# A matrix product by nested seven-product schemes: one more product in quarters, and two measures of b22 moved

## The chip, the cores and the metric

One core of a Trainium2 chip runs the whole kernel. The metric is the device time of that core in microseconds (us); lower is better. Times below are for one execution unless they are called a median.

## The reference

```
a, b: float32, 4096 x 4096;  alpha: 0.01
x = a @ b
out = where(x > 0, x, alpha * x)
```

## The kernel before

**Seven products instead of eight.** Both matrices are cut into regions of the output of 1024 x 1024. A region is named (g, j): g counts 1024 rows of A (0 to 3), j counts 1024 columns of B (0 to 3). Region (0,0) is computed plainly at the start. Each of the 15 others is computed by Winograd's form of Strassen's scheme: the rows are split into two halves h of 512, the columns into two halves nt of 512, and the inner dimension of 4096 into two halves of 2048, each of which is held as two tiles k. From these come seven products of a 512 x 2048 block with a 2048 x 512 block, in this order (`PRODUCTS`): a11, a12, s2, s3, s1, a22, s4 on the side of A, where s1 to s4 are sums of blocks of A made by VectorE once per g (`sum_a`; s3 is made in the place of the block a21). On the side of B the sums are made in every region by `b_sum` (line 575), in place. A product is `product(n, banks, first)`, line 789: 64 matmuls of 128x128 by 128x512, two tiles k, eight chunks c, four row tiles mt, into four PSUM banks. Banks y take products one, three, five and seven, banks z products two, four and six; between them the accumulated values are copied by ScalarE (`keep`, line 802) or added by VectorE (line 946) to tiles c in SBUF, passed through the leaky step (line 310) and stored by `leave`.

**Quarters.** In the regions with g > 0 that bring in no A (`in_quarters`), the sixth and seventh products are split once more by the same scheme, into seven quarter products of 16 matmuls of 128x128 by 128x256 (`quarter_product`, line 739), and in all of these but the first of a group (`in_fourth`) the fourth is too (`fourth_in_quarters`). A quarter product needs further sums. On the side of B they are made by VectorE in each region: `t3_of_b` (line 668, in place) and `sums_of_b` (lines 674, 676, 678: tq 2, 4 and 1). On the side of A they are made once per group: those of s4 and a22 in the group's first region (`sums_of_a`, line 688) and stored to DRAM (`kept_q`); those of s3 by `sums_of_s3` (line 722), three of which stay in the rooms of the quarters x21 of a22, s4 and s3 (`s3_rooms`), while the fourth, sx4, goes to DRAM (`kept_s3`). The quarters x21 that are overwritten in this way are stored first (`keep_x21`, line 704) and loaded back (`load_x21`, line 710) for the regions that use the whole blocks again.

**The order of regions.** Group 0: (0,1), (0,2), (0,3). Group 1: (1,2), (1,0), (1,3), (1,1). Group 2: (2,2), (2,0), (2,3), (2,1). Group 3: (3,2), (3,0), (3,1), (3,3). The last region of groups 0 to 2 also brings in A for the next group (`turning`). For each quadrant (h, half) of the next A, four pieces n are fetched by POOL's DMA queue (`fetch_a`, line 132, four DMAs of 128 KB for a piece, float32 rounded to float16 on the way), turned by VectorE (line 141), and squared by ScalarE for a measure of their range (`square_a`, line 594). The pieces pass through the pool a16, which has three buffers. A quadrant can be turned only when the block that it replaces has had its last product: (0,0) during product two, (0,1) during products three and four, (1,0) from product five on, (1,1) in product seven. Then VectorE makes the next s1 and s2 (line 545).

**Order and waits.** The order of instructions on each engine is the order of the program text (a manual schedule); each engine and each DMA queue runs its own list in order, and waits on semaphores. Tiles of a pool are reused in the order in which they come free. The pool x holds three large tiles, in turn s1, s2 and s4 of a group; in the regions in quarters the tile `q` takes the place of s2 after the third product, and s2 is loaded again from DRAM (`load_s2`).

**Measures.** The kernel checks the ranges of its inputs. For each block of B and A a `Measure` squares it on ScalarE in four parts (line 230) and sums and folds the squares on VectorE (lines 239 to 263). Where a measure stands is given by tables: `EARLY`, `MEASURED` (the entries: one in the middle of the first two products; a list of late ones after the third product; a fifth and a sixth for after those products) and `IN_ROOM`, for those that use the place of the next s2 instead of buffers of a16. The last region judges the statistics (`judge`); a result out of range would send the kernel into a plain loop at its end, which these inputs do not use.

Of the kernel before, what the change touches and what calls it, by code (L numbers as in the profile page):

```python
# [8 lines left out]
P = 128  # L9
DT = mybir.dt.float16  # L10
# [37 lines left out]
def kernel(  # L48
# [524 lines left out]
    def b_sum(to, x0, x1, op):  # L573
        f = lambda t: t.rearrange("p c n -> p (c n)")
        nc.vector.tensor_tensor(f(to), f(x0), f(x1), op)  # L575

    def measure(i, which, x, y, room=None):

        if which:
            tiles = [have_b[i, 2 * x + k, y] for k in ((1, 0) if regions[i][0] else (0, 1))]  # L580
        else:
            tiles = [at[regions[i][0], x, 2 * y + k] for k in range(2)]
        parts = halves(tiles[0]) + halves(tiles[1])
        if tiles[0] is first_a:
            return MeasureFirst(which, parts, None)
        return Measure(which, parts, not which, room)

    junk = small_pool.tile([P, NT], BF16, name="junk")
    rows_made = []
# [12 lines left out]
    def judge(line):  # L602
# [29 lines left out]
        (1, 0): [B11], (1, 3): [B11], (2, 0): [B12, B21], (2, 3): [B21], (2, 1): [B12], (3, 1): [B11, B21],  # L632
    }
    MEASURED = {
        (0, 1): (None, [A11], B12, B11), (0, 2): (B21, [B22, A22], B12, A12),
        (3, 0): (B22, [], None, None),
    }
    IN_ROOM = {(0, 3): B22, (1, 1): B22}

    PRODUCTS = [("a11", 0, 0), ("a12", 1, 0), ("s2", 0, 0), ("s3", 0, 1), ("s1", 0, 0), ("a22", 1, 0), ("s4", 1, 1)]  # L640

# [5 lines left out]
    kept_s2 = dram_pool.tile([2, P, KC * RM], DT, name="kept_s2")  # L647
    kept_q = {name: dram_pool.tile([4, P, QUARTER], DT, name=f"kept_q{name}") for name in ("a22", "s4")}
    kept_s3 = dram_pool.tile([P, QUARTER], DT, name="kept_s3")
    kept_x21 = {name: dram_pool.tile([P, QUARTER], DT, name=f"kept_x{name}") for name in ("a22", "s4", "s3")}  # L650
    side = 0

    def a_quarter(t):
# [72 lines left out]
    def s3_rooms(g):  # L726
        return {1: x21(g, "a22"), 2: x21(g, "s4"), 3: x21(g, "s3")}
# [5 lines left out]
    def quarter_product(xq, yq, to, first=False, by_row=False, banks=1):  # L733
        order = [(c, m) for c in range(KC) for m in range(2)]
        if by_row:
            order = [(c, m) for m in range(2) for c in range(KC)]
        for c, m in order:
            rows = slice(m * P, (m + 1) * P)
            nc.tensor.matmul(  # L739
                to[m], xq[:, c // 2, rows, c % 2], yq[:, c, :],  # L740
                start=first and c == 0 and m < banks, stop=c == KC - 1, skip_group_check=True,
            )
# [27 lines left out]
    for i, (g, j) in enumerate(regions):  # L770
# [33 lines left out]

        def fourth_in_quarters(banks, tq, sx):

            pairs, kept = new_c(side)
            b = quarters_of_b(i, 0, 1)
            x = quarters_of_a(g, "s3")
            one, other, third, fourth = banks  # L810
            t = lambda n: b_quarter(tq[n])
            block = lambda r, n: pairs[r][:, :, n * HALF:(n + 1) * HALF]
            quarter_product(x[0, 1], b[1, 0], into(fourth), True)
            quarter_product(x[0, 0], b[0, 0], into(one), True)
            nc.scalar.copy(block(0, 0), pair(one))
            quarter_product(sx[4], b[1, 1], into(other), True)
            quarter_product(x[1, 1], t(4), into(third), True)
            nc.scalar.copy(block(1, 0), pair(third))
            quarter_product(sx[2], t(2), into(one))
            nc.scalar.copy(block(0, 1), pair(one))  # L820
            quarter_product(sx[1], t(1), into(third), True)
            nc.scalar.copy(block(1, 1), pair(third))
            quarter_product(sx[3], b[0, 1], into(one))
            return pairs, kept, [(block(r, n), pair(bank)) for r, n, bank in (
                (0, 0, fourth), (0, 1, other), (0, 1, third), (1, 0, one), (1, 1, one))]

# [117 lines left out]
        def add(acc, banks):  # L944
            for to, bank in zip(acc, banks):
                nc.vector.tensor_add(to, bank, to)  # L946

        def leave(pairs, h, nt):
            for r, t in enumerate(pairs):
                leaky(t.rearrange("p m n -> p (m n)"))  # L950
                for m in range(2):
                    nc.sync.dma_start(place(g, h, 2 * r + m, j, nt), t[:, m, :])
# [19 lines left out]
        def square_a(h, half, n):  # L972
            square_rows(coming[h, half][n][1].held[0], n, coming["rows", h, half])
            if n == MT - 1:
                rows_made.append(coming["rows", h, half])

        def bring_a(h, half, some=range(MT)):
            if turning:
                for n in some:
                    fetch_a(h, half, n)  # L980
                    coming[h, half][n][1]()
                    square_a(h, half, n)

        y = [new_bank(ybank + mt) for mt in range(MT)]
        z = [new_bank(zbank + mt) for mt in range(MT)]
# [41 lines left out]
        if first_of_group:  # L1027
            sum_a(g, "s3")
            if g:
                sum_a(g, "s4")  # L1030
        if turning and g:
            load_x21(g, "s3")
        bring_a(0, 0, range(3 if g else 4))

        product(1, z, True)
# [19 lines left out]
            sum_a(g, "s4")  # L1055
        for k in ks:
            b_sum(B(1, 0, k), B(1, 0, k), B(0, 0, k), SUB)
        if first_of_group and g:
            keep_x21(g, "s3")
            keep_x21(g, "s4")  # L1060
            sums_of_a(g, "s4", new_a16)
        if not g:
# [3 lines left out]
        if late_ones:  # L1066
            late_ones[0].begin()
        u2_pairs, u2 = keep(y, 1 - side)
        if in_quarters:
            t = x_pool.tile([P, 4, QUARTER], DT, name="q", tag="x")  # L1070
        if in_fourth:
            tq[1] = t[:, 3]
            sums_of_b(quarters_of_b(i, 0, 1), tq, (1,))
        for k in ks:
            b_sum(B(0, 0, k), B(1, 1, k), B(0, 0, k), SUB)
        if g:
            bring_a(0, 1, range(3))
        if late_ones:
            late_ones[0].end()
        if in_quarters and first_of_group:  # L1080
# [2 lines left out]
            keep_x21(g, "a22")  # L1083

        z = [new_bank(zbank + mt) for mt in range(MT)]
        if in_fourth:
            v_pairs, v, parts = fourth_in_quarters(z, tq, {**s3_rooms(g), 4: a_quarter(sx4)})
            for to, bank in parts:
                nc.vector.tensor_add(to, bank, to)
            sq = {n: t[:, 3] if n == 4 else new_a16() for n in (1, 2, 3, 4)}  # L1090
            load_sums("a22", sq, (1, 2, 3, 4))
        else:
            product(3, z, True)
            v_pairs, v = keep(z, side)
        if in_quarters:
            tq = {2: t[:, 0], 1: t[:, 1], 4: t[:, 2]}
        fetch_b(i + 1, [(0, 1)], (1, 0) if in_fourth else ks)
        in_room = None
        if turning:
            room = new_s(g + 1, "s2").rearrange("p k c m e -> p (k c m e)").bitcast(BF16)  # L1100
            if (g, j) in IN_ROOM:
                in_room = measure(i, *IN_ROOM[g, j], room.rearrange("p (n w) -> p n w", n=4))
                in_room.begin()
                in_room.end()
            if g:
                bring_a(0, 1, [3])
            note_rows(1)
            for n in range(3):
                fetch_a(1, 0, n)
            coming[1, 0][0][1]()  # L1110
            square_a(1, 0, 0)
            fetch_a(1, 0, 3)
            load_x21(g, "a22")
            load_x21(g, "s4")
# [6 lines left out]
        if in_quarters:  # L1121
            t3_of_b(quarters_of_b(i, 1, 0))
            sums_of_b(quarters_of_b(i, 1, 0), tq)
            t3_of_b(quarters_of_b(i, 1, 1))
            for to, more in zip(u2_pairs, v_pairs):
                f = lambda t: t.rearrange("p m n -> p (m n)")
                nc.vector.tensor_add(f(to), f(to), f(more))
            if final:
                good = next(judged)

# [7 lines left out]
            leave(v_pairs, 1, 1)  # L1138
        if turning:
            for n in range(1, MT):  # L1140
                coming[1, 0][n][1]()
                square_a(1, 0, n)
            note_rows(1)
        if fifth:
            fifth = measure(i + 1, *fifth)
# [2 lines left out]
        fetch_b(i + 1, [(0, 0)], ks)  # L1148

        if not in_quarters:  # L1150
            product(5, z, False)
            add(u2[::-1], z[::-1])
        fetch_b(i + 1, [(1, 0)], (1, 0) if in_quarters else ks)
        bring_a(1, 1, range(3))
# [101 lines left out]
```

## Time and profile before

| what | before |
|---|---|
| median of 3 runs | 1549.6 us (1549.58 to 1549.91) |
| the profiled execution | 1550.65 us |
| its span, first to last instruction | 1548.9 us |
| PE (TensorE matmul) busy | 1530.1 us, 99% |
| DVE (VectorE) busy | 1138.8 us, 74% |
| ACT (ScalarE) busy | 425.1 us, 27% |
| mean granted TensorE clock | 0.997 |
| DMA, mean over the span | 222 GB/s |

A line of a timeline has start, duration, engine, line of the kernel, operation, output and input, shapes and count, and in brackets the idle time before it and what ended it. A line of waits has the waiting engine and line, whom it waited for, the total in us, how often and the longest. In the chain of waits each line has the start, the duration and the work that held the end at that time; "issue" is time for which the profile shows no wait. The start of a region can be read from the timeline of PE: (1,2) begins at 412.87, (1,1) at 699.70, (2,2) at 796.39, (2,1) at 1073.89, (3,2) at 1170.59 and (3,3) near 1448.14.

### The profile page before, as it was taken

The page shows a single profiled execution, that of the slowest core. Times are in us where ns is not written, and L with a number is a line of the kernel's source. Part 1 is how long each engine was busy: PE and PEld are TensorE (multiplying, and loading weights), DVE is VectorE, ACT ScalarE, POOL GpSimd, SP SyncE. Part 2 cuts the span into 40 slices and gives each one's busy share as a digit, 9 for nine tenths or more (in the row PEclk, how much of TensorE's full clock was granted, in tenths as well). Part 3 has the DMA queues.
Part 4 walks back from the last instruction along what each step waited for, and adds up shares of the span by engine and source line. Part 5 has one row for each costly group of instructions (what it writes and reads, how often), then busy time and mean ns, then how long its engine had stood idle before and what let it go on. Part 6 is the DMA issues. An engine that isn't in the chain of part 4 may idle for free.

```text
span 1548.9 us, 21600 instructions
## 1 busy us (share of the span) xinstructions
PE 1530.1 (99%) x8571; PEld 838.1 (54%) x8571; DVE 1138.8 (74%) x1179; ACT 425.1 (27%) x730; POOL 282.5 (18%) x458
## 2 busy tenths in 40 slices
PE   9999999999998999999999999999999999999997
PEld 4444444444445557574444747657444475746656
DVE  4368757767697786767669798686958768787486
ACT  2201224646510312103650041312543103041110
POOL 5641110142201011013220201110430110101100
PEclk9999999999999999999999999999999999999999
DMA  9999995997979969599798989959899895949934
GB/s 247 186 214 196 237 285 160 181 191 156 244 287 267 262 150 269 144 284 282 148 265 289 284 197 195 281 147 325 168 277 280 210 268 136 288 169 187 272 116 139
DMA packets 207361, 343.90 MB, mean 222 GB/s; under 512 B 18961, under 2 KB 150289, under 8 KB 197266
## 3 DMA queue, kind: packets, MB, share of 16 engines
q0 software_dynamic: 136704, 129.00, 52.4%
q1 hardware_dynamic: 63922, 187.86, 33.0%
q10 hardware_dynamic: 6624, 25.56, 4.5%
q8 instruction: 69, 1.13, 0.3%
q14 instruction: 42, 0.34, 0.1%
HBM read 361.76 MB, written 107.48 MB: 303 GB/s over the span
## 4 chain that ended last, share of the span: by engine, by line
PE 69%; DVE 3%; DMA 2%; ACT 1%; issue 1%; POOL 0%; DVEq 0%; ACTq 0%
PE ps L789 47%; PE ps L739 21%; DMA a<-in_a_dram 1%; DVE b L575 1%; DVE s L545 1%; DMA kept_qs<-q 0%; ACT junk L594 0%; ACT s L230 0%; DVE c L310 0%; DVE a L545 0%; DVE a L141 0%; DVE c L946 0%; DVE q L688 0%; POOL a L132 0%; DVE c L937 0%
## 5 line engine op out<-in xcount | busy, mean ns | idle before, releaser
L789 PE MATMUL ps<-b,a 128*128 128x512 f16 x2752 | 598.9, 379 | 0.4 <-DVE c L946 0.4
L789 PE MATMUL ps<-b,s 128*128 128x512 f16 x2240 | 491.8, 380 | 5.8 <-DVE b L575 5.8
L789 PEld LDWEIGHTS <-a 128*128 128x128 f16 x2752 | 269.2, 98 | 323.7 <-issue 1.2
L789 PEld LDWEIGHTS <-s 128*128 128x128 f16 x2240 | 219.7, 98 | 271.0 <-DVE b L575 6.3
L575 DVE TENSOR_TENSOR b<-b 128x4096 f16<-128x4096 f16 x104 | 234.9, 2287 | 64.1 <-DMA b<-in_b_dram 58.9
L519 POOL DMA_DIRECT2D b<-in_b_dram x160 | 118.8, 747 | 876.9 <-PE ps L739 316.8
L802 ACT COPY c<-ps 128x512 f32<-128x512 f32 x172 | 88.8, 595 | 477.0 <-PE ps L789 407.0
L141 DVE STREAM_TRANSPOSE a<-a 128x512 uint32<-128x512 uint32 (+2 forms) x120 | 126.8, 1104 | 90.5 <-DMA a<-in_a_dram 90.3
L132 POOL DMA_DIRECT2D a<-in_a_dram x252 | 137.7, 552 | 263.3 <-ACT junk L594 99.9
L594 ACT ACTIVATE junk<-a 128x512 bf16<-128x512 f16 x192 | 121.2, 631 | 89.7 <-DMA a<-in_a_dram 76.6
L739 PEld LDWEIGHTS <-q 128*128 128x128 f16 x1392 | 136.2, 98 | 15.8
L310 DVE SCALAR_TENSOR_TENSOR c<-c 128x1024 f32<-128x1024 f32 (+1 forms) x121 | 141.4, 1209 | 4.4 <-ACT c L802 4.2
L946 DVE TENSOR_TENSOR c<-ps,c 128x512 f32<-128x512 f32 x142 | 88.8, 682 | 59.7 <-PE ps L789 46.3
L230 ACT ACTIVATE sq<-b 128x2048 bf16<-128x2048 f16 x56 | 104.3, 1910 | 55.2 <-DVE sq L239 40.7
L282 PE MATMUL ps<-b,a 128*128 128x512 f16 x512 | 112.8, 379 | 1.9 <-DVE part L321 0.8
L739 PEld LDWEIGHTS <-a 128*128 128x128 f16 x1040 | 101.8, 98 | 15.4
L739 PE MATMUL ps<-b,q 128*128 128x256 f16 x752 | 88.1, 273 | 0.0
L282 PEld LDWEIGHTS <-a 128*128 128x128 f16 x512 | 49.7, 98 | 62.9 <-issue 3.0
L887 ACT COPY c<-ps 128x512 f32<-128x512 f32 x9 | 5.3, 587 | 277.1 <-PE ps L739 156.9
L739 PE MATMUL ps<-b,a 128*128 128x256 f16 x656 | 77.2, 273 | 0.0
L840 DVE TENSOR_TENSOR c<-ps,c 128x512 f32<-128x512 f32 x80 | 52.3, 684 | 15.9 <-PE ps L739 15.9
L739 PEld LDWEIGHTS <-s 128*128 128x128 f16 x592 | 57.9, 98 | 6.7
(112 smaller groups left out, 880.8 us busy)
## 6 DMA issues: line engine op xcount, KB each, us to landing
b<-in_b_dram POOLq DMA_DIRECT2D x168, 512.0 KB, 12.1
out_dram<-c SPq DMA_DIRECT2D x240, 256.0 KB, 5.8
a<-in_a_dram POOLq DMA_DIRECT2D x244, 128.0 KB, 5.7
b<-kept SPq DMA_DIRECT2D x20, 1024.0 KB, 8.9
q<-kept_qs ACTq DMA_DIRECT2D x40, 512.0 KB, 7.7
s<-kept_s SPq DMA_DIRECT2D x18, 1024.0 KB, 7.3
q<-kept_qa SPq DMA_DIRECT2D x28, 512.0 KB, 7.1
b<-kept_last SPq DMA_DIRECT2D x12, 1024.0 KB, 11.3
```

Source lines behind the costliest of these rows:

```text
L132: nc.gpsimd.dma_start(a16[32 * q:32 * q + 32], src.rearrange("(g i) w -> i g w", i=32))
L141: nc.vector.transpose(part.rearrange("p c m e -> p c (m e)").bitcast(U32) .rearrange("p c (g i) -> p g c i", i=32), src[:, :, i * n:(i + 1 ...
L230: nc.scalar.activation(to, self.parts[n], SQUARE)
L282: nc.tensor.matmul(ps, a_cols(at[0, h, u], c, mt, (h, u) == (0, 0)), bt[0, u, nt][:, c, :], start=first, stop=last,)
L310: nc.vector.scalar_tensor_tensor(t, t, alpha, t, op0=MULT, op1=MAX if alpha <= 1 else MIN)
L519: nc.gpsimd.dma_start(t[:, c:c + 4, :], b_rows(j, u, c, 4, nt, g > 0))
L575: nc.vector.tensor_tensor(f(to), f(x0), f(x1), op)
L594: nc.scalar.activation(junk, piece[:, q, :], SQUARE, accum_out=to[:, 4 * n + q:4 * n + q + 1])
L739: nc.tensor.matmul(to[m], xq[:, c // 2, rows, c % 2], yq[:, c, :], start=first and c == 0 and m < banks, stop=c == KC - 1, skip_group_chec ...
L789: nc.tensor.matmul(banks[mt], a_cols(t, c, mt, t is first_a), B(half, nt, k)[:, c, :], start=first and (k, c) == todo[0], stop=(k, c) == t ...
L802: nc.scalar.copy(kept[mt], banks[mt])
L946: nc.vector.tensor_add(to, bank, to)
```

## The change

- In the two later turning regions, (1,1) and (2,1), the fourth product is made of quarters too. The tile `q` is now taken in every region with g > 0; in these two it holds tq 2, 4, 1 and sx4, and is given back before the next group's s2 takes that room. sx4 is loaded from `kept_s3`; its quarter product is the last of the seven there. VectorE makes t3 and the three sums of B around the end of the third product, adds five blocks from PSUM to the tiles v afterwards, and adds v to u2 (`add_v`); the sixth product then starts afresh in its banks.
- The fetches of the pieces (0,1) 0 to 2 of the next A are issued before the third product, and are turned and squared after the fourth has been issued.
- x21 of s3 is no longer stored in the groups' first regions, nor loaded in (1,1) and (2,1).
- The two measures in the room of s2 (B22 in (0,3) and in (1,1)) are gone with `IN_ROOM`; B22 is measured as a second late one in (0,1), and in the middle of (3,3).

```diff
     MEASURED = {
-        (0, 1): (None, [A11], B12, B11), (0, 2): (B21, [B22, A22], B12, A12),
-        (3, 0): (B22, [], None, None),
+        (0, 1): (None, [A11, B22], B12, B11), (0, 2): (B21, [B22, A22], B12, A12),
+        (3, 0): (B22, [], None, None), (3, 3): (B22, [], None, None),
     }
-    IN_ROOM = {(0, 3): B22, (1, 1): B22}
...
@@ fourth_in_quarters
             nc.scalar.copy(block(0, 0), pair(one))
-            quarter_product(sx[4], b[1, 1], into(other), True)
+            if not turning:
+                quarter_product(sx[4], b[1, 1], into(other), True)
             quarter_product(x[1, 1], t(4), into(third), True)
...
             quarter_product(sx[3], b[0, 1], into(one))
+            if turning:
+                quarter_product(sx[4], b[1, 1], into(other), True)
...
+        def add_v():
+            for to, more in zip(u2_pairs, v_pairs):
+                f = lambda t: t.rearrange("p m n -> p (m n)")
+                nc.vector.tensor_add(f(to), f(to), f(more))
...
+        def turn_a_in(h, half, n):
+            coming[h, half][n][1]()
+            square_a(h, half, n)
...
-        if turning and g:
-            load_x21(g, "s3")
         bring_a(0, 0, range(3 if g else 4))
...
         for k in ks:
             b_sum(B(1, 0, k), B(1, 0, k), B(0, 0, k), SUB)
+        if turning and g:
+            t3_of_b(quarters_of_b(i, 0, 1))
+            for n in range(3):
+                fetch_a(0, 1, n)
         if first_of_group and g:
-            keep_x21(g, "s3")
             keep_x21(g, "s4")
...
         u2_pairs, u2 = keep(y, 1 - side)
-        if in_quarters:
+        if g:
             t = x_pool.tile([P, 4, QUARTER], DT, name="q", tag="x")
         if in_fourth:
             tq[1] = t[:, 3]
             sums_of_b(quarters_of_b(i, 0, 1), tq, (1,))
+        elif turning and g:
+            tq, sx4 = {2: t[:, 0], 4: t[:, 1], 1: t[:, 2]}, t[:, 3]
+            sums_of_b(quarters_of_b(i, 0, 1), tq, (2, 4, 1))
+            nc.sync.dma_start(sx4, kept_s3)
         for k in ks:
             b_sum(B(0, 0, k), B(1, 1, k), B(0, 0, k), SUB)
-        if g:
-            bring_a(0, 1, range(3))
...
-        if in_fourth:
+        if in_fourth or turning and g:
             v_pairs, v, parts = fourth_in_quarters(z, tq, {**s3_rooms(g), 4: a_quarter(sx4)})
+            if turning:
+                for n in range(3):
+                    turn_a_in(0, 1, n)
             for to, bank in parts:
                 nc.vector.tensor_add(to, bank, to)
+            if turning:
+                add_v()
...
         if turning:
-            room = new_s(g + 1, "s2").rearrange("p k c m e -> p (k c m e)").bitcast(BF16)
-            if (g, j) in IN_ROOM:
-                in_room = measure(i, *IN_ROOM[g, j], room.rearrange("p (n w) -> p n w", n=4))
-                in_room.begin()
-                in_room.end()
+            new_s(g + 1, "s2")
...
         if not in_quarters:
-            product(5, z, False)
+            product(5, z, g > 0)
             add(u2[::-1], z[::-1])
```

More of the change, by code (lines that the diff above doesn't have):

```diff
@@ L575, in b_sum, with measure @@
         nc.vector.tensor_tensor(f(to), f(x0), f(x1), op)
-    def measure(i, which, x, y, room=None):
+    def measure(i, which, x, y):
         if which:
@@ L585, in measure @@
             return MeasureFirst(which, parts, None)
-        return Measure(which, parts, not which, room)
+        return Measure(which, parts, not which)
     junk = small_pool.tile([P, NT], BF16, name="junk")
@@ L649 @@
     kept_s3 = dram_pool.tile([P, QUARTER], DT, name="kept_s3")
-    kept_x21 = {name: dram_pool.tile([P, QUARTER], DT, name=f"kept_x{name}") for name in ("a22", "s4", "s3")}
+    kept_x21 = {name: dram_pool.tile([P, QUARTER], DT, name=f"kept_x{name}") for name in ("a22", "s4")}
     side = 0
@@ L980, in bring_a @@
                     fetch_a(h, half, n)
-                    coming[h, half][n][1]()
-                    square_a(h, half, n)
+                    turn_a_in(h, half, n)
         y = [new_bank(ybank + mt) for mt in range(MT)]
@@ L1085 @@
         z = [new_bank(zbank + mt) for mt in range(MT)]
-        if in_fourth:
+        if in_fourth or turning and g:
             v_pairs, v, parts = fourth_in_quarters(z, tq, {**s3_rooms(g), 4: a_quarter(sx4)})
+            if turning:
+                for n in range(3):
+                    turn_a_in(0, 1, n)
             for to, bank in parts:
                 nc.vector.tensor_add(to, bank, to)
-            sq = {n: t[:, 3] if n == 4 else new_a16() for n in (1, 2, 3, 4)}
-            load_sums("a22", sq, (1, 2, 3, 4))
+            if turning:
+                add_v()
         else:
@@ L1094 @@
             v_pairs, v = keep(z, side)
+        if in_fourth:
+            sq = {n: t[:, 3] if n == 4 else new_a16() for n in (1, 2, 3, 4)}
+            load_sums("a22", sq, (1, 2, 3, 4))
         if in_quarters:
             tq = {2: t[:, 0], 1: t[:, 1], 4: t[:, 2]}
-        fetch_b(i + 1, [(0, 1)], (1, 0) if in_fourth else ks)
-        in_room = None
+        fetch_b(i + 1, [(0, 1)], (1, 0) if in_fourth else (0, 1) if turning and g else ks)
         if turning:
-            room = new_s(g + 1, "s2").rearrange("p k c m e -> p (k c m e)").bitcast(BF16)
-            if (g, j) in IN_ROOM:
-                in_room = measure(i, *IN_ROOM[g, j], room.rearrange("p (n w) -> p n w", n=4))
-                in_room.begin()
-                in_room.end()
+            new_s(g + 1, "s2")
             if g:
@@ L1109 @@
                 fetch_a(1, 0, n)
-            coming[1, 0][0][1]()
-            square_a(1, 0, 0)
+            turn_a_in(1, 0, 0)
             fetch_a(1, 0, 3)
@@ L1124 @@
             t3_of_b(quarters_of_b(i, 1, 1))
-            for to, more in zip(u2_pairs, v_pairs):
-                f = lambda t: t.rearrange("p m n -> p (m n)")
-                nc.vector.tensor_add(f(to), f(to), f(more))
+            add_v()
             if final:
@@ L1140 @@
             for n in range(1, MT):
-                coming[1, 0][n][1]()
-                square_a(1, 0, n)
+                turn_a_in(1, 0, n)
             note_rows(1)
```

## The prediction

> **What bounds the kernel now.** I read the page first, then who waits for whom on PE, then the PE timeline around the one long wait, then the chain of waits backwards from it.
>
> ```profile
> PE 1530.1 (99%) x8571; PEld 838.1 (54%) x8571; DVE 1138.8 (74%) x1179; ACT 425.1 (27%) x730; POOL 282.5 (18%) x458
> ```
>
> That is the page's busy time by engine; next, PE's longest wait (total, times, longest), and PE's timeline around it:
>
> ```profile
> PE ps L789 <- DVE b L575: 5.8, 1, 5.8
> ```
>
> ```profile
> 454.31 0.67 PE L789 MATMUL ps<-b,a 128*128 128x512 f16 x2
> ...
> 474.91 16.63 PE L789 MATMUL ps<-b,s 128*128 128x512 f16 x64 [5.78 <-DVE b L575]
> 491.38 1.91 PE L739 MATMUL ps<-b,a 128*128 128x256 f16 x16
> ```
>
> PE is the bound and waits long only once: 5.78 us before the fifth product of region (1,2). The clock was halved after it. In the table by windows (length, busy time of PE, PEld, DVE, ACT and POOL, then clock, DMA share, GB/s):
>
> ```profile
> 472.00:474.00 2.00, 0.00 (x0) 0.00 (x0) 2.00 (x2) 0.00 (x0) 0.34 (x1) 0.87 1.11 330
> 474.00:476.00 2.00, 1.09 (x3) 0.43 (x4) 2.00 (x2) 0.00 (x0) 0.00 (x0) 0.50 1.22 220
> ```
>
> The chain of waits says what made the wait, and gives the price of both kinds of product:
>
> ```profile
> 373.04 7.21 ACT s L230 x4
> 380.24 4.36 issue
> ...
> 395.35 17.07 DMA a<-in_a_dram
> ...
> 464.84 7.71 DMA kept_qs<-q
> 472.55 0.02 issue
> 472.57 2.30 DVE b L575
> 474.87 0.05 issue
> 474.91 16.63 PE ps L789 x64
> ...
> 557.44 12.23 PE ps L739 x112
> 569.66 13.81 PE ps L789 x64
> ```
>
> The chain begins with the four squares of the measure in region (0,3), runs through the fetch of A for the next group, then through DVE, hardly idle from 419.4 to 465.9, then through one store to DRAM whose buffer DVE needs, and ends in PE. A whole product is 13.81, one in quarters 12.23. DVE's wait for that store, in (1,2) and at the same place in (2,2):
>
> ```profile
> 471.43 1.23 DVE L688 TENSOR_TENSOR q<-s,q 128x2048 f16<-128x2048 f16 x1 [5.48 <-DMA kept_qs<-q]
> ...
> 842.19 1.23 DVE L688 TENSOR_TENSOR q<-s,q 128x2048 f16<-128x2048 f16 x1 [0.36 <-DMA kept_qs<-q]
> ```
>
> **1. The fourth product in quarters, regions (1,1) and (2,1).** On PE, 64 matmuls (13.81) become 112 half-wide ones (12.23): 1.58 each, **-3.16** for both. The chain has PE alone through both regions, so this counts in full if nothing new makes PE wait. What could:
> - Its operands. Products three to seven start 13.81 apart: in (1,1) the fourth begins at 741.14. The q tile may be written once the third product has read s2. DVE then makes tq 2 and 4 (1.22 each, L674 and L676) until 743.7, and the third quarter product, first to read t(4), begins two quarter products (2 x 1.747 = 3.49; 12.23 / 7 each) after the start, at 744.6. Slack 0.9. In (2,1) DVE is later: L575 at 1110.84, two of 2.21, then 1.22 for t3 (L668) and two sums of 1.25 end at 1119.0, with the reader due at 1115.33 + 3.49 = 1118.8: **+0.2**. The removed load of x21 of s3 could make this nothing, as DVE waited 1.75 in that stage for A while that load ran.
> - ACT copies bank `one` (0.59, L815) between its two products, which have one other product (1.747) between them: about 0.9 spare.
> - sx4 comes from DRAM on SP's queue, issued when product three ends. The same 512 KB load (L1044) landed in 4.0; it is read last, 10.5 after the start. Hidden.
> - Behind it on SP are the two loads of t3 for the next region, freed at 751.8 and 753.5 (before 748.24 and 755.5), and the x21 loads of a22 and s4, which must follow the last reader of their room. The a22 ones were issued at 755.52 and now at 753.9; they took about 9.9. They are wanted only in the second half of the sixth product, because the order of k is (1, 0): at 767.2 + 6.9. Hidden by 9 us in (1,1), and by 6 in (2,1), where the slowest of these loads took 12.4.
> - DVE gains 1.22 (t3), 3 x 1.22 (sums), 5 x 0.69 (L1089) and 2 x 1.22 (L1127): 10.8. Cover: in (1,1) the measure's 7.5 of work goes away, with a wait of 10.57; in (2,1) DVE waits 5.42, 6.30, 3.46 and 6.69 between 1125 and 1166. If that cover failed, the next group's A would be late (second rival).
> - ACT's 12 squares of A's (0,1) pieces go behind the four copies: from 742.6 to about 750.7. They free the buffers for POOL's fetches of (0,1,3), (1,0,0), (1,0,1), which so start up to 8 us later. The (1,0) pieces 1 to 3 are turned after the fifth product ends in any case (L946, then L310, then L141), now 1.58 earlier, so I take 0 on the path.
>
> **2. The measure leaves (0,3).** ACT loses 4 squares (7.34), DVE the adds and folds up to 384.2. ACT's wait of 4.36 before its next squares ended when DVE's stats (L600, 384.18, behind that measure) were done. So POOL's fetch of piece (1,0,3) goes from 387.88 to about 376, into a stage with a DMA share of 0.07, and DVE's adds (L946, 386.46) can begin as the product ends, 384.9: 1.6 earlier, and so the turn at 391.09 and the fetch of (1,1,0) at 393.74. That fetch took 18.8 to the first turn (412.54). In (2,1), where (1,0,3) had landed before, it took 1166.15 - 1149.89 = 16.3. The chain gets between 1.6 and 1.6 + 2.5 = 4.1 earlier; I take 3.5, because the overlap that (2,1) lacks is what goes away.
>
> **3. Group 1's x21 of s3 is not stored.** DVE's fourth sum waited 5.48 for the store of the first (463.58 to about 471.3, 7.7 us), with two x21 stores ahead and POOL's b loads from 462.52. In the two later groups, with no b loads at that time, the same wait was 0.36 and 0.40. Now one x21 store is gone and the first sum is stored 3.5 earlier, at 460.1, before the b loads, which PE releases. The wait is bounded by 0.4 and 5.48; I take 0.4, the nearest rows: 5.1 gained.
>
> **Sum for the wait.** Without the two small waits on z at 455, product four would end at 454.31 + 13.81 = 468.12. B's first half was ready at 474.9. To lose the whole wait it must come 6.8 earlier; 3.5 + 5.1 = 8.6, slack 1.8. Gain: 491.38 - 454.31 = 37.07 for two products that take 27.62: **-9.45**, of which 2.66 is the slow clock and 0.84 the small waits. With 1.6 and half of the store's wait gone, 2.5 of waiting remain; with 1.6 and none of it gone, 5.2. How long a wait halves the clock the trace leaves open: 0.22 did not, 5.78 did, the clock falling about 4.4 after the last matmul. So a rest of 2.5 costs between 2.5 and 5.2. The Trainium skill, "TensorE: Matmul & The Clock Gate" (section "What's actually happening"), puts the limit at one idle window of about 3.4 us, free-running; by it a rest of 2.5 would cost its 2.5 alone, and a rest of 5.2 the slow clock too. No run here shows a wait between the two.
>
> **4. Measures of B22 in (0,1) and (3,3).** In (0,1) ACT's squares follow the copies at 183, and DVE's 7.1 (in (3,0): 1291.49 to 1298.60) lie in an idle 5.77 before 191.47, so its adds are up to 3 late; their banks are next written by the seventh product, near 205.5. Hidden. In (3,3) the 7.1 goes between L575 (ends 1476.4) and L946. The store, and behind it the load of sx4 (L1044 at 1482.0), move to 1489.1 and land at 1493.1; its quarter product begins at 1489.58 + 3.49 = 1493.07. **+0.2**. DVE's tq 1 (L678) is then ready near 1497.2, and is read at 1489.58 + 5 x 1.747 = 1498.3; if the loads of b came 1 later than they did, that cover would be gone and each further us would cost one.
>
> Total: -3.16 - 9.45 + 0.2 + 0.2 = -12.2. From the profiled execution's 1550.65 (span 1548.9) this makes 1538.4; that run lies 1.05 above the median 1549.6, so for the median **1537.4**.
>
> **Rivals.**
> - *Part of the wait in (1,2) stays* (the store is slow again, or the DMA stage at 393 to 412 gains only the 1.6). For it: the DMA share is at 1.0 and over all through that stage. Against it: both later groups wait 0.4 at this store. With 1 to 5.2 left, the latter with the slow clock: 1538.4 to 1545.3; likeliest 1540. Chance 0.2.
> - *The next A comes late, slower.* The 8 us that ACT loses in the turning regions runs through the three a16 buffers into the fetch of A's last quarter. Today s2 is ready at 817.9 for a product at 824.02 (6.1 spare) in (2,2), and at 1186.3 for 1198.2 (11.9) in (3,2); PE comes 1.6 earlier, so 4.5 and 10.3 are spare. A delay D costs (D - 4.5) + (D - 10.3) + 2 x 2.66 for the clock; it decides the sign at D near 11. With 8 us and 5 more from DMA, D = 13: 16.5 lost against 12.2, so 1554. Against it: the turns of (1,0) are tied to the end of product five, and (1,1) gives back a measure. Chance 0.08.
> - *Small waits on t(4), the copy or x21 in both turning regions*, 1 to 3 us each, no more: the slack of 0.9 is thin. 1539.4 to 1543.4. Chance 0.1.
> - *The wait in (1,2) stays whole*, the chain being held by DMA alone: 1537.4 + 9.45 = 1546.9, which is 0.17% under today's. Chance 0.04.
>
> **Numbers.** My forecast has 0.58. The forecast and those parts of the first and third rivals that end by 1543 hold over 8 in 10; below, only the two +0.2 and a little scatter can fall away: 1536 to 1543. A difference under 0.2% (3.1 us) can't be told from none. Faster: 0.58 + 0.2 + 0.1 = 0.88; within it, the last rival: 0.04; slower: 0.08.
>
> **What would show it.** Right: the fourth product of (1,1) and (2,1) as 112 matmuls in 12.23 with no idle; PE's wait for L575 gone and the clock at 1.00 around 470; DVE's fourth sum waiting under 1 us for kept_qs; the fetch of (1,1,0) in (0,3) at about 392 and its turn near 409. Wrong: a PE wait for q in L739 over 1 us, a wait for s2 (DVE L545) in (2,2) or (3,2), or the L575 wait still over 2 us.

## The result, and the profile after

The changed kernel takes 1540.14 us (median of six runs, 1537.96 to 1541.79), beside 1549.76 for the kernel before on the same chip (six runs, 1548.43 to 1553.57): a ratio of 0.9934, 95% interval 0.9921 to 0.9947. It is faster by 9.6 us. The prediction was 1537.4, with a range of 1536.0 to 1543.0, so the time lies inside the range, 2.7 us above the forecast: the gain is 9.6 us where 12.2 was forecast. The profiled execution took 1540.23, with a span of 1538.1.

The page's line of busy times shows what the quarters do: 96 more matmuls on PE (2 x 48), and 22 more instructions on DVE.

```profile
PE 1524.4 (99%) x8667; PEld 846.8 (55%) x8667; DVE 1158.1 (75%) x1201; ACT 426.0 (28%) x730; POOL 281.9 (18%) x458
```

In PE's waits of the changed kernel the long one for L575 is gone, and one in region (1,2) is new. PE's timeline through the fourth, fifth and sixth products of (1,2): the fifth now follows the fourth without a gap, and the new wait stands in the sixth.

```profile
454.60 13.98 PE L788 MATMUL ps<-b,a 128*128 128x512 f16 x64
468.41 13.98 PE L788 MATMUL ps<-b,s 128*128 128x512 f16 x64
...
491.77 1.91 PE L738 MATMUL ps<-b,q 128*128 128x256 f16 x16 [0.65 <-DVE c L843]
```

The table by windows has the clock at full speed in the fifth product, whose first microseconds ran at half clock before (columns: length, busy time of PE, PEld, DVE, ACT, POOL, then clock, DMA share, GB/s):

```profile
470.00:474.00 4.00, 4.00 (x20) 1.79 (x19) 2.68 (x3) 0.02 (x1) 0.74 (x1) 1.00 1.12 309
```

On DVE, the fourth sum of s4 waits 1.30 for the store in place of 5.48, but two of a22's sums, which did not wait before, now do:

```profile
464.69 1.23 DVE L687 TENSOR_TENSOR q<-s,q 128x2048 f16<-128x2048 f16 x1 [1.30 <-DMA kept_qs<-q]
...
472.68 1.23 DVE L687 TENSOR_TENSOR q<-q,a 128x2048 f16<-128x2048 f16 x1 [1.22 <-DMA kept_qs<-q]
474.70 1.23 DVE L687 TENSOR_TENSOR q<-a 128x2048 f16<-128x2048 f16 x1 [0.80 <-DMA kept_qs<-q]
```

From there the chain of waits is PE alone to the last products. Its pieces at 733.10 and 1105.71 are the fourth products of (1,1) and (2,1), now in quarters:

```profile
491.77 15.88 PE ps L738 x144
...
733.10 12.23 PE ps L738 x112
...
1105.71 12.23 PE ps L738 x112
...
1294.33 12.38 PE ps L738 x112
```

Where the time went, by the starts of regions on PE (kernel before, then changed): (1,2) starts at 412.87 and 413.16, +0.29 before the changed part of the chain has acted; (1,2) itself lasts 102.97 and 94.33, -8.64; the stretch from (1,0) to (1,1) +0.15; (1,1) 96.69 and 95.10, -1.59; (2,2) to (3,2), with the other product in quarters, -1.59; (3,2) to (3,3) +0.16, of which 0.15 is in the piece of 12.38 above. The last matmul ends 11.22 earlier (1539.21 and 1527.99) and the span 10.8.

### The profile page after: what moved, and what is told of

Its sections match the earlier page's. It is cut to its first block, busy times and chain, and to the rows that moved or that the text cites. A ratio compares the mean times of both kernels' runs of the same rounds, so it can differ in the third digit from the quotient of the medians.

```text
span 1538.1 us, 21821 instructions
## 1 busy us (share of the span) xinstructions
PE 1524.4 (99%) x8667; PEld 846.8 (55%) x8667; DVE 1158.1 (75%) x1201; ACT 426.0 (28%) x730; POOL 281.9 (18%) x458
## 4 chain that ended last, share of the span: by engine, by line
PE 67%; DVE 1%; issue 0%; DVEq 0%
PE ps L788 45%; PE ps L738 22%; DVE c L310 0%; DVE c L949 0%; DVE c L843 0%; DVE c L940 0%; DVE c L954 0%; DVE b L667 0%; DVEq L940 0%
## 5 line engine op out<-in xcount | busy, mean ns | idle before, releaser
L788 PE MATMUL ps<-b,a 128*128 128x512 f16 x2624 | 570.8, 379 | 0.0
L575 DVE TENSOR_TENSOR b<-b 128x4096 f16<-128x4096 f16 x104 | 235.1, 2289 | 65.4 <-DMA b<-in_b_dram 56.7
L801 ACT COPY c<-ps 128x512 f32<-128x512 f32 x164 | 84.6, 596 | 452.1 <-PE ps L788 365.0
L738 PEld LDWEIGHTS <-q 128*128 128x128 f16 x1424 | 139.3, 98 | 16.9 <-issue 0.8
L230 ACT ACTIVATE sq<-b 128x2048 bf16<-128x2048 f16 x64 | 119.1, 1909 | 57.6 <-DVE sq L239 41.8
L282 PE MATMUL ps<-b,a 128*128 128x512 f16 x512 | 112.8, 379 | 2.1 <-DVE part L321 0.9
L738 PE MATMUL ps<-b,q 128*128 128x256 f16 x784 | 92.1, 273 | 0.6 <-DVE c L843 0.6
L738 PE MATMUL ps<-b,a 128*128 128x256 f16 x752 | 88.3, 273 | 0.0
L890 ACT COPY c<-ps 128x512 f32<-128x512 f32 x9 | 5.3, 586 | 269.9 <-PE ps L738 120.2
```

Source lines behind the costliest of these rows:

```text
L230: nc.scalar.activation(to, self.parts[n], SQUARE)
L282: nc.tensor.matmul(ps, a_cols(at[0, h, u], c, mt, (h, u) == (0, 0)), bt[0, u, nt][:, c, :], start=first, stop=last,)
L738: nc.tensor.matmul(to[m], xq[:, c // 2, rows, c % 2], yq[:, c, :], start=first and c == 0 and m < banks, stop=c == KC - 1, skip_group_chec ...
L788: nc.tensor.matmul(banks[mt], a_cols(t, c, mt, t is first_a), B(half, nt, k)[:, c, :], start=first and (k, c) == todo[0], stop=(k, c) == t ...
L801: nc.scalar.copy(kept[mt], banks[mt])
```

## The experiments

The prediction put the wait in (1,2) down to a store that was slow since two stores of x21 and then the loads of B went beside it, and to a chain through A's fetch that could come 3.5 us earlier. The changed kernel alters both. Each kernel below stands against the kernel before, run on the same chip.

**The two measures moved, nothing else** (`measures_only`): the kernel before with the new tables. Both stores of x21 stay.

```diff
-        (0, 1): (None, [A11], B12, B11), (0, 2): (B21, [B22, A22], B12, A12),
-        (3, 0): (B22, [], None, None),
+        (0, 1): (None, [A11, B22], B12, B11), (0, 2): (B21, [B22, A22], B12, A12),
+        (3, 0): (B22, [], None, None), (3, 3): (B22, [], None, None),
...
-    IN_ROOM = {(0, 3): B22, (1, 1): B22}
+    IN_ROOM = {}
```

> The kernel before with only the tables of measures of the changed kernel: B22 in (0,1) and (3,3), none in the room of s2; products, stores and loads as before. Theory (two supplies: the chain that begins in (0,3) comes 2.5 us earlier by the measure's leaving, and the store of the first sum lands sooner because no x21 of s3 is ahead of it): DVE's first sum of s4 (L688) starts near 459.8 to 461 instead of 462.3, its store is queued behind both x21 stores, so the fourth sum still waits 2 to 3.5 us (5.48 before, 1.30 in the changed kernel); PE's wait for L575 in (1,2) is 1 to 2.5 us and the clock is not halved; 7 to 9 us faster than before. Rival (the chain alone counts, the x21 store is nothing): the fourth sum waits about 1.3, PE does not wait, 9 us faster. Second rival (the x21 store alone counts): PE still waits 3 us or more and the clock is halved, 1 to 3 us faster.

1542.07 us beside 1549.99, ratio 0.9945 (0.9929 to 0.9962): 7.9 of the 9.6 us. The fourth sum, with two x21 stores still ahead of its store:

```profile
461.05 1.23 DVE L688 TENSOR_TENSOR q<-s,q 128x2048 f16<-128x2048 f16 x1 [0.37 <-DMA kept_qs<-q]
```

Moving the measures takes the wait away with no store left out. The prediction's third step gave 5.1 us to the store that is left out and the earlier start together; for the store's part there is no support here. One thing stays open: the first sum of s4 starts at 457.07 here, 5.3 us earlier than before, a larger lead than in any profile of the changed kernel (459.77, 458.88 and 458.07), and no run keeps that store with the smaller lead.

**The store of x21 of s3 moved behind the four stores** (`x21_s3_later`), in the kernel before.

```diff
         if first_of_group and g:
-            keep_x21(g, "s3")
             keep_x21(g, "s4")
             sums_of_a(g, "s4", new_a16)
+            keep_x21(g, "s3")
```

> The kernel before, with the store of x21 of s3 queued on SP behind the four stores of the sums of s4 instead of ahead of them; same bytes, same measures. Theory: the first sum is still stored at 463.6, after POOL's b loads at 462.5, but half a megabyte less is ahead: the fourth sum waits about 4 instead of 5.48, PE 4.3 to 4.8 instead of 5.78; 1 to 4 us faster, by whether the clock is halved. Rival (the chain alone counts): wait and time as before within 1 us. Second rival (the x21 store alone counts): the fourth sum waits about 1.3, PE under 2, 5 us or more faster.

1549.51, ratio 0.9993 (0.9983 to 1.0003). The fourth sum, and PE behind it with a wait of 5.30, are as late as ever:

```profile
470.51 1.23 DVE L688 TENSOR_TENSOR q<-s,q 128x2048 f16<-128x2048 f16 x1 [4.99 <-DMA kept_qs<-q]
```

So this x21 store ahead is not what delays the first sum's store by 5 us.

**One measure back at a time, in the changed kernel** (`measure_back_03`, `measure_back_11`): B22 in the room of s2 again in (0,3), and not in (3,3); or in (1,1), and not in (0,1). The cut is of the first:

```diff
...
     MEASURED = {
...
-        (3, 0): (B22, [], None, None), (3, 3): (B22, [], None, None),
+        (3, 0): (B22, [], None, None),
...
+    IN_ROOM = {(0, 3): B22}
...
-            new_s(g + 1, "s2")
+            room = new_s(g + 1, "s2").rearrange("p k c m e -> p (k c m e)").bitcast(BF16)
+            if (g, j) in IN_ROOM:
+                in_room = measure(i, *IN_ROOM[g, j], room.rearrange("p (n w) -> p n w", n=4))
+                in_room.begin()
+                in_room.end()
```

> The changed kernel with the measure of B22 back in the room of s2 in (0,3) and none in (3,3); the rest as changed: quarters in (1,1) and (2,1), no x21 of s3. Theory: s1 of the next A starts near 423.9 again (421.4 in the changed kernel), the store is issued after the b loads, the fourth sum waits about 4, PE 4 to 4.8; the quarters give their 3.16; 4 to 7 us faster than before. Rival (the chain alone counts): PE waits 5.8 with the slow clock, 3.2 us faster. Second rival (the x21 store alone counts): PE waits under 2, 8 us or more faster. In all cases the fourth products of (1,1) and (2,1) take 12.23.

1547.41, ratio 0.998 (0.9966 to 0.9995): 2.6 us of gain are left, close to the 3.16 of the two products in quarters, and the wait is back in full although the x21 store of s3 is gone:

```profile
469.74 1.23 DVE L688 TENSOR_TENSOR q<-s,q 128x2048 f16<-128x2048 f16 x1 [5.04 <-DMA kept_qs<-q]
```

> The changed kernel with the measure of block B22 in region (1,1) in the room of the next s2, and none in (0,1). It tests whether the quarters need the measure's leaving there. Theory (cover is ample): ACT's four squares (7.3) come behind the 12 squares of A, DVE's adds behind add_v, so that the pieces (0,1,3) and (1,0,0) are turned some 4 us later and the fetch of (1,1,0) some 3.5 later; s2 of group 2, ready 6.3 us before its product in the changed kernel, is ready 2 to 3.5 before it; no PE wait, the same time as the changed kernel within 1 us (about 10 faster than before). Rival (the next A comes late): PE waits for s2 (DVE L545) or for L575 in (2,2), 1 to 5 us, 5 to 9 faster than before.

1542.89, ratio 0.9947 (0.9931 to 0.9964), 2.7 to 3.7 us above the changed kernel's medians, which are from other chips. The loss is at a place that the prediction did not name. PE's timeline in the second product of (2,2), and the clock behind it:

```profile
801.27 11.02 PE L789 MATMUL ps<-b,a 128*128 128x512 f16 x40 [2.16 <-ACT c L802]
```

```profile
802.00:803.00 1.00, 0.89 (x3) 0.21 (x2) 1.00 (x2) 1.00 (x3) 0.00 (x0) 0.60 1.05 354
803.00:804.00 1.00, 1.00 (x4) 0.33 (x3) 1.00 (x1) 0.97 (x4) 0.00 (x0) 0.50 1.05 279
```

That product needs the banks that ACT copies out after the seventh product of (1,1), and those copies (800.66, done at 802.68) stand in ACT's queue behind twelve squares of the next A. The first of these squares waits for A's last pieces, and so starts at 791.73 here, against 787.98 in the changed kernel, whose copies are done at 798.92 for a product that begins at 800.4. The cover is 1.5 us there.

**The loads of B for the next region started later** (`before_b_later`, `after_b_later`): a tiny copy on GpSimd in (1,2), behind the fourth product.

```diff
+        if g == 1 and first_of_group:
+            nc.gpsimd.tensor_copy(x[:, :1], v[0][:, :1])
         fetch_b(i + 1, [(0, 1)], ...)
```

> The kernel before with one tiny copy on GpSimd in the first region of the second group, (1,2), which reads the fourth product's copied result: the loads of b12 for the next region, queued behind it on GpSimd, start when the fourth product has ended (at about 470 us) and not in its middle (462.5). Both stores of x21 stay where they are, and DVE's chain of s1 and s2 is not earlier. Theory (the first store of kept_qs is late since it shares the DMA engines with those loads): the fourth sum's wait falls from 5.48 us to under 1.5, the fifth product's wait from 5.8 to under 2, and the time falls by 5 to 9 us, to 1541 to 1545. Rival (only DVE's earlier chain, through something else than these loads, takes the wait away): the wait stays near 5 us and the time at 1549 to 1550. Second rival (the stores on SP and x21 are what is slow): also unchanged.

The sums of the kernel before, with every x21 store in place and the first sum's store issued at 462.7:

```profile
466.06 1.23 DVE L688 TENSOR_TENSOR q<-s,q 128x2048 f16<-128x2048 f16 x1 [1.01 <-DMA kept_qs<-q]
```

The wait went from 5.48 to 1.01, and PE's before the fifth product from 5.78 to 1.31: the loads of B are what made the store late. The DMA view of 464 to 466 us shows how. In the kernel before, GpSimd's queue with the loads holds the DMA engines while SP's queue with the stores (q1) moves 0.02 MB; in `before_b_later` q1 has them to itself (packets, MB, share of 16 engines; the kernel before first):

```profile
q0 software_dynamic: 194, 0.20, 96.5%
```

```profile
q1 hardware_dynamic: 220, 0.81, 102.0%
```

But the time was 1550.93, ratio 1.0008 (0.9998 to 1.0017). At the start of the next region, (1,0), PE met the same delay again:

```profile
510.63 1.89 PE L789 MATMUL ps<-b,a 128*128 128x512 f16 x8 [2.65 <-DMA b<-in_b_dram]
515.42 24.94 PE L789 MATMUL ps<-b,a 128*128 128x512 f16 x107 [2.90 <-DMA b<-in_b_dram]
```

I had priced the mechanism and not the delay of the loads itself.

> The kernel after with the same tiny copy on GpSimd in (1,2). Theory: the fourth sum's wait falls from 1.30 us to about 0.4, but the loads that are later now share the DMA engines with the stores of a22's sums (467 to 478 us): if the waits of 1.22 and 0.80 there go too, PE's wait of 0.65 in the sixth product goes, and the time is 0.5 to 1 us below the changed kernel's; if they grow, it is up to 2 us above it. Rival (loads play no part): all waits and the time are as in the changed kernel.

1547.34, ratio 0.9984 (0.9974 to 0.9994), 8 us above the changed kernel: PE waits 6.80 for b at 512.99. Outside both expectations, for the same reason. The fourth sum's wait missed its expectation too: it was 2.34 and not 0.4, though the loads of B began only at 469.65. So what is left of this wait in the changed kernel need not come from those loads; what makes it is not shown.

**A room of its own for the fourth sum** (`before_room4`, `after_room4`): loads, stores and measures stay, and only the wait's cause, the shared room, goes.

```diff
-            sums_of_a(g, "s4", new_a16)
+            if g > 1:
+                sums_of_a(g, "s4", new_a16)
...
             t = x_pool.tile([P, 4, QUARTER], DT, name="q", tag="x")
+        if first_of_group and g == 1:
+            sums_of_a(g, "s4", lambda n: t[:, 0] if n == 4 else new_a16())
```

> The kernel before, but in (1,2) the fourth sum of s4's quarters gets a room of its own (the first quarter of the tile named q, which is free then) in place of the room of the first sum, so it no longer waits for the first store of kept_qs; the loads of B, the stores and the measures stay as they were. Theory (the whole 9 us is the fourth sum standing behind that store, however the store came to be late, and the fifth product behind it): no wait at the fourth sum, the fifth product starts within 1 us of the fourth's end at full clock, a22's sums may wait 0 to 2 us for the same stores, and the time falls by 6 to 8.5 us, to 1541 to 1544. Rival (the late loads of B bound the next region anyway, as in the run that delayed them): PE waits for b at the start of (1,0) and the time falls by under 3 us.

The rival's forecast held: 1549.38, ratio 0.9994 (0.9981 to 1.0007). DVE's fourth sum runs at 466.24 without a wait and the fifth product waits 0.21, yet in (1,0):

```profile
509.06 1.89 PE L789 MATMUL ps<-b,a 128*128 128x512 f16 x8 [0.27 <-DMA b<-in_b_dram]
514.69 27.75 PE L789 MATMUL ps<-b,a 128*128 128x512 f16 x120 [3.74 <-DMA b<-in_b_dram]
542.27 13.98 PE L789 MATMUL ps<-b,s 128*128 128x512 f16 x64
```

The region starts 6.8 us earlier than in the kernel before (509.06 and 515.84); its third product starts 1.2 earlier (542.27 and 543.46). The wait in front of the fifth product had hidden a second bound: the first tiles of B for (1,0) arrive only then.

> The changed kernel with the same room of its own for the fourth sum. The wait of 0.55 to 1.4 us before that sum goes; by the theory PE gains only what it lost later in (1,2), 0 to 0.65 us, so the time is 0 to 0.7 us below the changed kernel's, about 1539.5. If waits for the stores come back in a22's sums in full, nothing is gained.

1539.60, ratio 0.9930 (0.9917 to 0.9944); the changed kernel on that chip 1539.27, ratio 0.9931. No wait is left at any of the eight sums in (1,2), and nothing is gained.

**The other x21 store moved behind the four stores, in the changed kernel** (`x21_s4_later`), the edit of `x21_s3_later` done with `keep_x21(g, "s4")`.

> The changed kernel with the one store of x21 that is left (s4's) queued on SP behind the four stores of kept_qs. If x21 ahead of the stores takes any part, the fourth sum's wait falls below 0.55 us; if it takes none, the wait stays in the 0.55 to 1.4 us of the changed kernel's runs. Time as the changed kernel's within 0.7 us by both.

1544.08, ratio 0.9958 (0.9945 to 0.9972), and a spread from 1539.2 to 1550.2. The fourth sum's wait was 2.41, not below 0.55, so the store ahead takes no part that can be seen (the changed kernel on this chip, below, has 2.43). The time was expected to stay, and rose by 4.8 us. PE in (1,0) again:

```profile
513.21 27.41 PE L788 MATMUL ps<-b,a 128*128 128x512 f16 x120 [3.91 <-DMA b<-in_b_dram]
```

A 512 KB store that went at 456, ahead of the loads of B, went at 467 instead, beside them. The edit moves the store in all three groups; most of the waiting it adds, 3.91 us and the slow clock behind it, is in (1,0).

**The changed kernel again** (`changed_again`, `changed_third`), on the chips of those two sets of runs.

> The changed kernel itself, to compare with the others of this call on one chip: 1538 to 1542 us.

> The changed kernel itself on the chip of this call, for comparison: 1538 to 1542 us; fourth sum's wait 0.5 to 1.4 us, and PE's wait in the sixth product of (1,2) 0 to 0.65 us.

1539.20 and 1539.27, ratios 0.9928 (0.9915 to 0.9941) and 0.9931 (0.9917 to 0.9945): 11.1 and 10.5 us below the kernel before on these chips, beside 9.6 in the first result. The fourth sum's wait is 0.55 and 2.43 there (the second beyond the 1.4 expected), beside 1.30 in the first profile, and PE's wait in the sixth product is gone in both: that 0.65 is scatter and no fixed cost.

**Two more sums on DVE ahead of the fifth product** (`extra_dve_2`), to see what a short rest of PE does to the clock.

```diff
+        if g == 1 and first_of_group:
+            for _ in range(2):
+                nc.vector.tensor_tensor(b_quarter(t[:, 0]), B(1, 1, 0)[:, :, :HALF], B(1, 1, 0)[:, :, HALF:], ADD)
```

> The changed kernel with two more sums of a quarter on DVE (1.22 us each, their results overwritten) ahead of the sum of B in (1,2) that the fifth product waits for: PE should rest 2.0 to 2.3 us there. If the clock is halved after a rest of that length, as it was for 3.41 us after 2.16 us in the run with the measure back in (1,1), the region grows by about 2.2 + 1.7 = 3.9 us; if that clock had another cause, by 2.2 alone, with the clock at 1.00.

One run of 1541.94, 2.7 above the changed kernel on that chip. PE rested 2.28 and the clock stayed at 1.00, so the rest cost its length alone, as in the second expectation:

```profile
470.93 13.99 PE L788 MATMUL ps<-b,s 128*128 128x512 f16 x64 [2.28 <-DVE b L575]
```

```profile
470.00:474.00 4.00, 3.07 (x15) 1.41 (x16) 4.00 (x3) 0.10 (x1) 0.74 (x1) 1.00 1.12 309
474.00:478.00 4.00, 4.00 (x20) 1.83 (x19) 3.97 (x5) 0.00 (x0) 0.00 (x0) 1.00 1.25 219
```

**What ties these together.** GpSimd's queue brings the B tiles of (1,0). The bytes that it moved between 455 and 507 us, shortly before they are wanted, sort the kernels that reach (1,0) early. The line of that queue in the DMA view of this stretch (packets, MB, share of 16 engines), for `measures_only`, then the changed kernel, then `before_room4`, then `before_b_later`:

```profile
q0 software_dynamic: 4723, 4.70, 55.6%
```

```profile
q0 software_dynamic: 4283, 4.26, 50.9%
```

```profile
q0 software_dynamic: 3870, 3.85, 46.6%
```

```profile
q0 software_dynamic: 3473, 3.46, 41.9%
```

PE's waits for b at the start of (1,0) are 0, 0, 4.0 and 5.5; `x21_s4_later` (3.89 MB) waits 3.9, `after_b_later` (3.29 MB) 6.8, and all other runs with the earlier chain (4.27 to 4.63 MB) wait 0 to 0.6. (The kernel before, with 4.32 MB, begins (1,0) only at 515.84 and has less other traffic in that stretch, since everything behind its fifth product comes later.) What the earlier chain does is seen in the windows. In the kernel before, the DMA engines are nearly idle from 452 to 457, until DVE has made what is to be stored:

```profile
447.00:452.00 5.00, 5.00 (x25) 2.29 (x24) 5.00 (x3) 0.00 (x0) 0.00 (x0) 1.00 1.01 419
452.00:457.00 5.00, 4.56 (x21) 1.89 (x20) 5.00 (x7) 2.05 (x4) 0.00 (x0) 1.00 0.10 41
```

In `measures_only` that gap comes 5 us sooner, and the stores behind it run in the second window:

```profile
447.00:452.00 5.00, 5.00 (x25) 2.25 (x23) 5.00 (x7) 0.00 (x0) 0.00 (x0) 1.00 0.07 30
452.00:457.00 5.00, 5.00 (x25) 2.26 (x24) 5.00 (x3) 2.06 (x4) 0.00 (x0) 1.00 0.92 326
```

At 326 against 41 GB/s for 5 us, 1.4 MB more of what follows the gap have left by 457 (what stands ahead of it has merely moved forward too), while the loads of B, which PE releases, begin at 461 to 462.5 in both. The stores are then out of the way of the loads, and the loads out of the way of the first sum's store. That the two bounds exist is shown by `before_b_later` and `before_room4`, which take away the first and meet the second; that the earlier chain lifts both at once is shown by `measures_only`, where (1,2) lasts 93.52 in place of 102.97. That it does so by this emptied queue is read from the bytes and not shown: no run moves the stores alone to an earlier time.

## Why the prediction was right, step by step

**Step 1, the quarters: right, to a hundredth.** 12.23 twice with no idle matmul, -1.59 measured for -1.58. In (2,1) the +0.2 for t(4) did not occur, and the hidden parts stayed hidden: s2 for (2,2) was ready at 807.9 for a product at 814.23, 6.3 spare. The second rival (next A late) is refuted; its cover did not shrink.

**Step 2, the measure leaving (0,3): right, within a scatter of its own size.** The fetch of (1,1,0) was forecast for 392 and the turn for 409. One line of GpSimd's timeline of the changed kernel, and two of DVE's:

```profile
392.45 4.29 POOL L132 DMA_DIRECT2D a<-in_a_dram  x8 [13.81 <-issue]
...
409.61 2.11 DVE L141 STREAM_TRANSPOSE a<-a 128x512 uint32<-128x512 uint32 x2 [7.57 <-DMA a<-in_a_dram]
...
421.41 4.45 DVE L545 TENSOR_TENSOR s<-a,a 128x4096 f16<-128x4096 f16 x2
```

The fetch took 17.2 to its first turn, between the 18.8 of before and the 16.3 of (2,1); s1 came at 421.41 in place of 423.95, 2.5 earlier for the 3.5 taken. In the three profiles of the changed kernel the first sum of s4 starts at 459.77, 458.88 and 458.07, beside 462.33: 2.6, 3.5 and 4.3 earlier, close to the bounds of 1.6 to 4.1 that the prediction gave. In `measures_only`, with the same edit for this step, it was 5.3, outside them.

**Step 3, the x21 store: the wrong cause.** The step said that the store left out, together with an earlier start, would take the wait from 5.48 to 0.4. The wait did fall, to between 0.55 and 2.43; the sign that the prediction named, under 1 us, was met in one of three profiles. But with that store still there it fell as far (`measures_only`, 0.37), and without it and the earlier chain it stayed (`measure_back_03`, 5.04). The half of the step's sentence that held is "before the b loads": `before_b_later` shows that their overlap makes the 5 us. For the same reason the chance for rival one, where part of the wait stays, was priced on the wrong ground.

**The sum for the wait: right in size, with luck at a bound that it did not contain.** It asked only whether B's first half for the fifth product came 6.8 earlier, and gave -9.45. (1,2) gave -8.64; 0.65 of the difference is the wait that came next, in the sixth product, for DVE, late by 1.22 and 0.80 at a22's sums. In `changed_again`, without that wait, (1,2) lasts 93.52, which is the -9.45. I had not asked what is late next on DVE, nor on GpSimd's queue. There the whole gain could have been lost: had the same wait been removed by another edit, as in `before_room4`, the sum would have said the same -9, and the result was -0.4, no difference clear of noise. That the earlier chain of the changed kernel kept this second bound away too was luck: the sum did not look there.

**Step 4: right that it is hidden.** The +0.2 in (3,3) did not occur: that region lasts 91.07 in both. The measure that leaves (1,1) was counted only as cover on DVE (its 7.5 us), not on ACT: putting it back costs 2.7 to 3.7 us (`measure_back_11`), through ACT's queue. The sum is unhurt only because the changed kernel keeps 1.5 us of cover there.

**The clock.** The rest of 2.5 us was priced between 2.5 and 5.2, since the trace left open how long a wait halves the clock. A rest of 2.28 (`extra_dve_2`) did not, nor did one of 2.65 (`before_b_later`) in the 1.9 us of work that followed it. Rests of 2.16 (`measure_back_11`), 2.90 (`before_b_later`, just behind that of 2.65), 3.74 (`before_room4`) and 3.91 (`x21_s4_later`) did, each for 3.41 us, and those of 5.30, 5.34, 5.78 and 6.80 for 6.83. The lower price of the prediction thus occurs (2.28), and so does a rest of about that length that loses 1.7 us to the clock besides (2.16, half of 3.41); the 2.66 that the upper price took from the kernel before goes with the longer spell, seen for rests of 5.30 and more. The Trainium skill, "TensorE: Matmul & The Clock Gate" (section "What's actually happening"), has free-running windows of 3413 ns: the lengths of 3.41 and 6.83 agree with one and two of them. The limit that the Trainium skill gives there for the slow clock, at least one idle window of about 3.4 us, is not what these runs show, as 2.16 was enough once; by that limit `measure_back_11` would have lost 1.7 us less, an estimate.

**From PE to the time.** PE came out at -11.22 for the forecast -12.2: +0.29 in the start of (1,2), +0.8 in (1,2), +0.3 in two small waits, less the 0.4 that did not occur. The medians differ by 9.6 where the profiled executions differ by 10.42; the one of before lay 0.9 above its median.

## What to carry to other kernels

Before a wait is put down as gain, look at every queue that runs on during it, DMA loads for the next stage above all: a bound that the wait now hides may be met soon after, and removing the wait then gains only the distance to that bound (0.4 us in `before_room4`). An engine's chain that ends in stores is also a gate for the DMA engines, so making it earlier can be worth more than making the store that one waits for shorter. And a measure or copy on an engine that is 28% busy can still be the last to free a bank, if it stands in order behind work that waits for a transfer.

## What the runs showed of the hardware that was not expected

- A 512 KB store to DRAM landed 3.2 us after its issue (median of four, `before_b_later`) with no loads of B beside it, and 7.8 with them (kernel before). Without them it was not always so short: 4.6 in `after_b_later`. From 464 to 468 in the kernel before, where stores and loads overlapped, all queues together moved 80 to 140 GB/s, with a DMA share of 0.99 to 1.13, against 401 to 418 from 464 to 467 in `before_b_later`, where the stores ran by themselves.
- Queuing one such store behind four others in each group, 11 us later, with nothing else changed, cost 4.8 us, most of it at a place 46 us on in the first, and widened the spread of the runs from 1.2 to 11 us.
- The slow clock came in spells of 3.41 or 6.83 us, and of two rests a little over 2 us one started such a spell (2.16) and one did not (2.28).
